# A two-layer hybrid backbone block: the order of instructions taken from another simulation in the framework

## The chip, the cores and the metric

The kernel runs on one core of one Trainium2 chip. The metric is the device time in microseconds (us) of one execution. Three executions of the kernel before gave 1864.18, 1868.44 and 1869.16 us; their median is 1868.44.

## The reference

Two layers run over 512 latent tokens and 256 context tokens of width 1024. In each layer the tokens are normalised and modulated, go through one input projection, and are mixed by four groups of heads side by side; the outputs are concatenated and projected, then a squared-ReLU MLP of width 4096 follows. Layer 2 drops the context after the mixing. Cut to what matters:

```python
for l in range(2):
    mx, mc = modulation(c, ...), modulation(c_ctx, ...)          # 6 rows of 1024 each
    px, pc = norm(x) @ w_in[l], norm(xc) @ w_in[l]               # 1024 -> 3344 columns
    gdn = gated_delta_net(pc, px)       # chunks of 64: a triangular solve, then a chain over chunks, both directions
    sc  = short_conv(px)                # gate * conv3(gate * x)
    hy  = hyena(px)                     # x0 * longconv(x1 * v), filters from a small MLP, by a Fourier transform
    na  = neighbourhood_attention(pc, px)   # softmax over a window and the context
    x = x + mx[2] * norm(concat(gdn, sc, hy, na) @ w_out[l])
    x = x + mx[5] * norm(square(relu(norm(x) @ w1[l])) @ w2[l])
    # layer 1 does the same for the context
```

## The kernel before, in words

Every large product is made of three matmuls on values that are split into a high and a low part (`mm3`, L135 to L140). A weight block of 128x512 comes by DMA into one of three `raw` buffers (`raw`, L116), ScalarE writes its high part `whi` (L126) and VectorE its low part `wlo` (L127), each in a ring of four. `big` (L146) makes one block of 128 output columns of the input projection or of the first MLP product: 12 matmuls of 512 columns on PSUM tile `mx` and 12 of 256 on `mc` for every such weight block in layer 1.

The stages of a layer follow each other in the source, and in the main in the trace:

1. Hyena: `hyena_project`, the filter spectra (`spectrum`, `spectra`; GpSimd makes `ha` at L472 and L473, and the matmuls of L508 and L521 read it), `hyena`.
2. DeltaNet, preparation: `gdn_rates`, `gdn_project` for k and q (each block goes through `dwconv`, L377 to L386, on ScalarE and VectorE), `gdn_normalise`.
3. DeltaNet, solve: `gdn_solve`. `gdn_inverse` (L853) first gathers the diagonal blocks (L866) and transposes them (L870), then runs 30 rounds of a product and an addition on VectorE (L886 and L888), each waiting for the one before it; `gdn_levels` builds the rest of the inverse with small matmuls (L932 to L981). As fill for TensorE, `values()` traces three blocks of the attention's projection (`na_project`, GpSimd splits them at L1137 and L1138) and the projection of v behind `gdn_inverse`.
4. DeltaNet, chain: `gdn_run` steps both directions of `gdn_chain` (L988 to L1088) in turn, six chunks each, across TensorE, ScalarE, VectorE and GpSimd.
5. `gdn_gate` and the rest of `na_project`, then `na_heads` (scores, softmax, values), `gdn_out`, `short_conv`.
6. `mlp`: the output projection, the norm, and the MLP in 11 groups of blocks.

The rows of the modulation are one more stream, spread over all of layer 1: `mod_steps` (L247) loads a 512 KB block of weights (L254) and reduces it on VectorE with up to four multiply-and-accumulate instructions (L258); 80 blocks in all. `step_mods` traces so many of them at chosen places, and in the MLP `mods` (L1403) ties each behind a given VectorE instruction with `issue_after`.

What sets the order: the source traces the instructions with the framework's tile context. When the context closes (L1709, L1710), the framework's scheduler plays the traced program on a simulated machine. Whenever an engine of that machine can take an instruction, it takes, among those whose inputs and buffers are ready by simulated time, the one traced first. The order in which each engine took its instructions becomes the order in the program, and the chip keeps it: an instruction whose inputs are late holds up all behind it on its engine or queue. Where the source says `issue_after`, an instruction stays behind a named one. SyncE's one queue (SP) issues all DMAs in such a fixed order. The framework has two simulated machines: a plain one, used without an argument, and a timeline simulation, which its own text calls the more detailed of the two.

## Time and profile before

| | |
|---|---|
| runs | 1864.18, 1868.44, 1869.16 us, median 1868.44 |
| profiled execution | 1861.5 us; its span 1859.7 us |
| busy | TensorE (PE) 1772.7 us, 95%; its weight loads (PEld) 1436.0; VectorE (DVE) 1267.8; ScalarE (ACT) 774.3; GpSimd (POOL) 263.1 |
| mean granted TensorE clock | 0.986 of full speed |
| DMA | 233.55 MB, 126 GB/s mean |

The span runs from the first to the last instruction; 1.8 us of the execution lie outside it. Matmuls are pipelined, so a busy PE row says that PE had work, not that it ran at its peak. A wait is put down to the engine whose semaphore came last. The granted clock is 1.00 at the upper of TensorE's two levels and 0.5 at the lower, averaged over a stretch.

### The profile page before, as it was taken

The numbers are of one execution on the slowest core, as the hardware profiler recorded it, in microseconds if no ns is written. First come the engines' busy times: TensorE is split into PE (matmuls) and PEld (weight loads), VectorE is DVE, ScalarE is ACT, GpSimd is POOL, SyncE is SP. The second block draws the span as 40 slices with busy tenths as digits, with TensorE's granted clock in tenths as the row PEclk, the third lists the DMA queues.
The fourth block names the chain that finished last, engine by engine and source line by source line (L and its number), as shares of the span: only waits on it lengthen the run. The fifth ranks groups of instructions, "written<-read, shape, count | busy, mean of one in ns | idle before, by whom it ended". The sixth has DMA issues, their size and how long they took to land. (4 is left out here: it accounts for less than half of the span.)

```text
span 1859.7 us, 29504 instructions
## 1 busy us (share of the span) xinstructions
PE 1772.7 (95%) x11170; PEld 1436.0 (77%) x11170; DVE 1267.8 (68%) x2366; ACT 774.3 (42%) x1548; POOL 263.1 (14%) x273
## 2 busy tenths in 40 slices
PE   6899888999999999999999999988899999999998
PEld 2667777788889888888888866777687787777776
DVE  5889898767776777655555586789756765544545
ACT  6333643466565222212222363463347662332323
POOL 0202531600120000000000041162330110000002
PEclk9999999999999999999999999999999999999999
DMA  8452213353565443433444233212235653322322
GB/s 300 150 182 97 91 63 114 118 147 124 182 212 170 146 129 117 123 124 114 130 125 131 83 141 111 69 60 91 73 103 152 210 182 98 106 98 78 115 80 85
DMA packets 105346, 233.55 MB, mean 126 GB/s; under 512 B 13202, under 2 KB 18132, under 8 KB 103925
## 3 DMA queue, kind: packets, MB, share of 16 engines
q1 hardware_dynamic: 105204, 231.68, 38.4%
q8 instruction: 88, 1.44, 0.3%
q14 instruction: 54, 0.43, 0.1%
HBM read 208.42 MB, written 23.21 MB: 125 GB/s over the span
## 5 line engine op out<-in xcount | busy, mean ns | idle before, releaser
L126 ACT CAST whi<-raw 128x512 fp32r<-128x512 f32 x444 | 273.6, 620 | 666.9 <-PE pb L140 269.8
L127 DVE TENSOR_TENSOR wlo<-raw,whi 128x512 fp32r<-128x512 f32 x444 | 317.1, 720 | 216.2 <-ACT whi L126 210.1
L140 PE MATMUL pb<-acth,wlo 128*128 128x512 f32 (+2 forms) x808 | 282.1, 349 | 0.2 <-DVE wlo L127 0.2
L139 PE MATMUL pb<-actl,whi 128*128 128x512 f32 (+2 forms) x808 | 281.8, 349 | 0.0
L138 PE MATMUL pb<-acth,whi 128*128 128x512 f32 (+2 forms) x808 | 280.9, 348 | 0.0
L138 PE MATMUL pb<-whi,hid 128*128 128x512 f32 x628 | 249.7, 398 | 0.8 <-ACT whi L126 0.6
L139 PE MATMUL pb<-wlo,hid 128*128 128x512 f32 x628 | 248.6, 396 | 0.3 <-DVE wlo L127 0.2
L140 PE MATMUL pb<-whi,hid 128*128 128x512 f32 x628 | 248.7, 396 | 0.0
L1498 DVE TENSOR_TENSOR acc<-acc,pb 128x1024 f32<-128x1024 f32 x96 | 117.2, 1221 | 152.6 <-PE pb L140 151.5
L258 DVE SCALAR_TENSOR_TENSOR junk<-adrow,cbc 128x512 bf16<-128x512 f32 x256 | 181.7, 710 | 6.0 <-DMA adrow<-in_adaD_dram 2.9
L139 PE MATMUL mx<-actl,whi 128*128 128x512 f32 x416 | 172.3, 414 | 1.4 <-POOL actl L374 1.2
L140 PE MATMUL mx<-acth,wlo 128*128 128x512 f32 x416 | 171.7, 413 | 0.5 <-DVE wlo L127 0.4
L138 PE MATMUL mx<-acth,whi 128*128 128x512 f32 x416 | 168.8, 406 | 2.1 <-ACT acth L235 1.2
L138 PEld LDWEIGHTS pb<-acth,whi 128*128 128x128 f32 x808 | 152.1, 188 | 20.4
L140 PEld LDWEIGHTS pb<-acth,wlo 128*128 128x128 f32 x808 | 152.0, 188 | 20.1 <-DVE wlo L127 0.4
L139 PEld LDWEIGHTS pb<-actl,whi 128*128 128x128 f32 x808 | 151.8, 188 | 20.1
L374 POOL TENSOR_TENSOR actl<-et,acth 128x256 fp32r<-128x256 f32 (+2 forms) x64 | 56.2, 896 | 732.7 <-DVE et L373 728.5
L138 PEld LDWEIGHTS pb<-whi,hid 128*128 128x128 f32 x628 | 117.8, 188 | 33.0 <-ACT hid L1399 5.4
L140 PEld LDWEIGHTS pb<-whi,hid 128*128 128x128 f32 x628 | 117.8, 188 | 29.5 <-DVE hid L1400 1.8
L139 PEld LDWEIGHTS pb<-wlo,hid 128*128 128x128 f32 x628 | 117.8, 188 | 28.3 <-DVE wlo L127 1.1
L138 PEld LDWEIGHTS mx<-acth,whi 128*128 128x128 f32 x416 | 79.5, 191 | 19.1 <-ACT acth L235 1.6
L139 PEld LDWEIGHTS mx<-actl,whi 128*128 128x128 f32 x416 | 79.7, 192 | 18.3 <-POOL actl L374 1.9
(398 smaller groups left out, 3015.3 us busy)
## 6 DMA issues: line engine op xcount, KB each, us to landing
raw<-in_w_dram SPq DMA_DIRECT2D x276, 256.0 KB, 2.8
adrow<-in_adaD_dram SPq DMA_DIRECT2D x80, 512.0 KB, 3.7
raw<-in_win_dram SPq DMA_DIRECT2D x104, 256.0 KB, 2.6
raw<-in_wout_dram SPq DMA_DIRECT2D x64, 256.0 KB, 3.0
X<-xdr SPq DMA_DIRECT2D x14, 512.0 KB, 4.4
X<-in_xin_dram SPq DMA_DIRECT2D x12, 512.0 KB, 5.1
xdr<-X SPq DMA_DIRECT2D x10, 512.0 KB, 2.8
adp<-in_adaP_dram SPq DMA_DIRECT2D x16, 256.0 KB, 5.5
```

The lines of the kernel that those rows point to most:

```text
L126: self.nc.scalar.copy(hi, raw)
L127: self.nc.vector.tensor_sub(lo, raw, hi.bitcast(F32))
L138: mmul(o, st[0], mv[0], start=first, stop=False)
L139: mmul(o, st[0], mv[1], start=False, stop=False)
L140: mmul(o, st[1], mv[0], start=False, stop=last)
L258: nc.vector.scalar_tensor_tensor(self.junk, raw[:, hs], 1.0, self.cbc[:, cnd, hs], op0=OP.mult, op1=OP.mult, accum_out=self.part[:, l, cnd ...
L374: nc.gpsimd.tensor_sub(lo[:, r], t, hi[:, r].bitcast(F32))
L1498: op = nc.vector.tensor_add(o, o, ps)
```

## The change

The tile context is opened with one more argument. Nothing that is traced changes: not an instruction, a tile, a buffer count, a priority or an `issue_after`. The scheduler plays the same traced program on the framework's timeline simulation in place of its plain one, and the order of every engine and of the DMA queue comes from there.

```diff
-    with tile.TileContext(nc) as tc:
+    with tile.TileContext(nc, schedule_with_timeline_sim=True) as tc:
         Net(tc, aps).run()
```

## Rows read from the trace of the kernel before

**Rows 1.** Busy time of each engine by stage, from the windows: x counts instructions.
```profile
0.00:60.00 60.00, 44.07 (x201) 21.06 (x201) 35.00 (x90) 35.81 (x66) 7.54 (x12) 1.00 0.78 283
60.00:250.00 190.00, 172.85 (x1032) 137.93 (x1031) 169.04 (x324) 82.92 (x182) 56.61 (x38) 0.97 0.33 115
250.00:326.00 76.00, 66.66 (x946) 57.14 (x947) 67.90 (x109) 25.59 (x45) 12.53 (x11) 0.91 0.31 102
326.00:372.00 46.00, 43.67 (x642) 36.68 (x639) 32.83 (x87) 18.67 (x37) 28.79 (x42) 1.00 0.38 115
372.00:558.00 186.00, 183.25 (x1097) 151.69 (x1096) 131.54 (x287) 118.75 (x256) 25.18 (x32) 1.00 0.53 166
558.00:1069.00 511.00, 511.00 (x2555) 429.59 (x2554) 325.99 (x663) 143.84 (x272) 0.00 (x0) 1.00 0.41 126
1069.00:1210.00 141.00, 130.92 (x657) 99.69 (x657) 102.48 (x163) 65.09 (x126) 35.18 (x32) 0.96 0.30 106
1210.00:1340.00 130.00, 113.06 (x1243) 93.55 (x1241) 114.48 (x177) 58.77 (x132) 45.74 (x40) 0.95 0.23 78
1340.00:1534.00 194.00, 188.31 (x1453) 154.74 (x1453) 124.80 (x249) 121.17 (x251) 40.22 (x61) 1.00 0.50 156
1534.00:1813.00 279.00, 278.79 (x1189) 222.27 (x1188) 139.70 (x183) 87.44 (x148) 0.00 (x0) 1.00 0.30 96
1813.00:1860.00 47.00, 40.08 (x175) 31.65 (x174) 24.09 (x40) 16.27 (x36) 11.31 (x8) 0.96 0.24 84
```

**Rows 2.** What PE waited for: us in total, times, longest us.
```profile
PE mc L138 <- DVE cv L385: 10.1, 2, 5.2
PE zp L932 <- DVE diagT L897: 7.9, 2, 4.4
...
PE dps L508 <- POOL ha L472: 5.8, 2, 3.0
...
PE dps L521 <- POOL ha L472: 2.9, 1, 2.9
```

**Rows 3.** VectorE's groups of instructions from 251 to 297 us, layer 1's solve.
```profile
L886 DVE TENSOR_TENSOR prod<-sys 128x60 f32<-128x60 f32 (+14 forms) x30 | 16.6, 553 | 0.7
L888 DVE TENSOR_TENSOR sys<-sys,prod 128x60 f32<-128x60 f32 (+14 forms) x30 | 15.7, 525 | 0.8
L127 DVE TENSOR_TENSOR wlo<-raw,whi 128x512 fp32r<-128x512 f32 x9 | 6.2, 689 | 1.4 <-ACT whi L126 1.3
```

**Rows 4.** VectorE in order of time, where the recurrence begins.
```profile
250.69 0.72 DVE L383 SCALAR_TENSOR_TENSOR cv<-mx,conv,cv 128x511 f32<-128x511 f32 x1
251.32 0.26 DVE L886 TENSOR_TENSOR prod<-sys 128x60 f32<-128x60 f32 x1
251.48 0.75 DVE L385 SCALAR_TENSOR_TENSOR cv<-mx,conv,cv 128x511 f32<-128x511 f32 x1
252.13 0.26 DVE L888 TENSOR_TENSOR sys<-sys,prod 128x60 f32<-128x60 f32 x1
```

**Rows 5.** The modulation's accumulations (L258) around the solve: window, length, VectorE busy.
```profile
250.00:297.00 47.00, 0.00 (x0) 0.92 0.26 89
326.00:372.00 46.00, 13.85 (x32) 1.00 0.38 115
```

**Rows 6.** What the DMA queue (SP) waited for: us in total, times, longest us.
```profile
SPq L118 <- DVE wlo L127: 757.4, 385, 11.7
...
SPq L629 <- DVE ub L628: 47.6, 6, 17.9
SPq L1133 <- ACT na L1131: 45.5, 4, 15.4
```

**Rows 7.** A table load on ScalarE and the instruction behind it, in order of time.
```profile
252.31 1.28 ACT L644 ACT_TABLE_LOAD   x1 [5.90 <-DVE cv L385]
253.60 0.63 ACT L644 ACTIVATE cv<-cv 128x512 f32<-128x512 f32 x1
```

## The prediction

> **What bounds the kernel now.** I read the windows by stage first. PE is busy for 1772.65 of the 1859.7 us, so it idles for 87, and the rows say where: 511.00 busy of 511 in layer 1's MLP and 278.79 of 279 in layer 2's, 790 us in which the order can save nothing; 15.9 idle at the start, where DMA moves 283 GB/s; 17.2 from 60 to 250; 9.3 and 2.3 in layer 1's solve and chain; 2.8 up to the MLP; 10.1, 16.9 and 5.7 in layer 2's three stretches before its MLP; 6.9 at the end [rows 1]. The granted clock is 1.00 but for 0.97 and 0.91 from 60 to 326, 0.96 and 0.95 from 1069 to 1340 and 0.96 at the end: TensorE is at its lower level for part of the stretches in which it also idles [rows 1]. In those stretches VectorE has little room: 169.04 of 190, 67.90 of 76, 114.48 of 130 us busy [rows 1].
>
> Then the list of PE's waits, to see whether the present order makes PE wait for something late while other work stands ready. The longest are few and are true dependences at the borders of stages: 10.1 us in two waits for `dwconv` (VectorE was gathering the inverse's diagonals first), 7.9 for the transposed result of the recurrence, 5.8 and 2.9 for GpSimd's `ha` [rows 2]. That is 26.7 us of the 87, and the trace shows no crowd of short, misplaced waits behind them.
>
> **The change part by part.** Nothing is added or removed; all instructions, DMAs and buffers stay. Only the order can move, and it can move on every engine and on SP's queue. The trace of before can't show the new order, so each place where two streams share an engine gets a bound from both sides and a value.
>
> (a) The recurrence on VectorE. It is what ends last in the solve: 30 products of 16.6 us and 30 additions of 15.7 in layer 1, 32.3 us of work in the 44 us from its first to its last instruction, and in between come other VectorE instructions, of which nine `wlo` of 0.69 are the largest group with 6.2 us [rows 3]. They alternate one by one with the links of the chain, because at each link the other stream was ready when the next link was not [rows 4]. So what the new simulation says about readiness decides how many slip in. From below: all others out, 44 - 32.3 = 11.7 us less per layer, 23 us in both, if PE still has fill. From above: the modulation's accumulations, of which none runs in the solve now and 16 (with their 16 accumulator reads 13.85 us) run right behind it [rows 5], all move in, +13.9 us, in layer 1 alone, and nine more `wlo` in each layer, 2 x 6.2, +26.3 together. I take half of the 16 accumulations, +6.9, and three more `wlo` in layer 2, 3 x 0.69 = +2.1; the choice lies toward the upper end because a lower-placed instruction that is ready is always taken and never held back for a link that will be ready soon. What is behind the recurrence is `diagT`, and PE already waits for it (7.9 us in the two layers [rows 2]): a later recurrence comes out at PE's wait nearly whole.
>
> (b) The border stalls. From below all 26.7 us go [rows 2]; from above they double. I take 0: these waits are for results which the traced priorities put late (the diagonals before `dwconv`), and the priorities don't change.
>
> (c) SP's queue. Loads wait for a free `raw` buffer as a rule (757.4 us in 385 waits), and some stand behind a store whose data is late, 17.9 us at the longest behind `ub`, 15.4 behind `na` [rows 6]. In the present order this costs PE next to nothing in the MLPs, as the four `whi`/`wlo` pairs cover it. Below: 0, there is nothing to win there. Above: if the ring runs dry as in the stretch from 1340 to 1534, where PE idles 5.7 of 194 us [rows 1], 2.9% of 790 us, 23 us. I take 0, the MLP's own row.
>
> (d) Start, chain, attention and end. PE idles 15.9 + 2.3 + 2.8 + 5.7 + 6.9 us there [rows 1]. Some 10 us of the start are loads that no order hides; I let these stand at 0, between -10 and +10, for either order fills the chain from the same projections.
>
> (e) Loads of activation tables. Each costs ScalarE 1.28 us, and the next ACTIVATE starts 1.29 us after the load did [rows 7]. An order that lets a Silu or a square root in among the exponentials pays twice for each visit. There are six such visits to the attention stage (four Silu of the gates, two square roots in `gdn_out`), 12 loads, 15.4 us of ScalarE, in stretches where it is busy for 118.75 of 186 and 121.17 of 194 us [rows 1]: cover for all of it. I take 0, -2 to +5. The Trainium skill ("ScalarE: Activation LUTs", section "What ACT_TABLE_LOAD costs") puts a switch at 1283 ns plus a drain of about 1380, 2.66 us together; by that the 12 would be an estimated 32 us. This trace agrees with the first figure and shows no drain between the load and the next instruction.
>
> The sum: 1861.5 + 6.9 + 2.1 = 1870.5 for an execution like the profiled one, which was 6.9 us below the median of the three runs; carried to the median, **1877 us**, 0.5% slower.
>
> **The rivals.** A change within 0.3%, 5.6 us, is about what can't be told from none.
>
> *Faster.* The new simulation's times fit the chip better, so that the fill arrives where PE now waits. For it: the waits of 5 us each for `dwconv` are the same at the same place in both layers [rows 2], a sign of a systematic error rather than of chance, and TensorE's clock falls in the same stretches. Against it: PE has only 87 us of idle time, of which the start, the end and the MLPs hold 23, and VectorE is busy for 88 to 89% where the rest is [rows 1]. If the two waits for `dwconv` and half of the other border waits go (10.1 + 8.3), it is 1868.4 - 18 = 1850.
>
> *No difference that counts.* The order differs only where it is free to differ, or not at all where the long chains and PSUM buffers tie it; then the argument does not do what it says. For it: 790 us are PE-bound, and the traced priorities stay. Against it: the alternation in the recurrence depends on ready times of tenths of a us [rows 4]. 1868 us.
>
> *Much slower.* The fill is put ahead of the chain of the solve in both layers: the one mechanism is a VectorE or PE queue which holds ready low-priority instructions when a link of the chain becomes ready. For it: the links already wait for one 0.7 us instruction each [rows 4]; against it: one is the rule in the trace and most of the 60 links wait for none. Each of the 60 links behind one `wlo` would be 60 x 0.69 = 41 us a layer less the 11.7 that are there now; with half of the links so, in both layers, 2 x (20.7 - 11.7) = 18, with PE's fill used up early, so that the chain of 46 us behind it (43.67 busy, part of it fill [rows 1]) runs uncovered at +10 a layer: 38 in all, 1907 us. It decides from the point at which more than a third of the links wait.
>
> **How the numbers follow.** Forecast, slower by 0.3 to 1.5%: 0.35, its own range 1874 to 1896. Faster: 0.31. No difference: 0.24. Much slower: 0.10. So faster 0.31, within 0.3% 0.24, slower 0.45. The range: 1868.4 - 23 = 1845 is the sum with the whole lower bound of (a) and nothing else, and a fifth of the faster case I put below 1843; from above, the upper bounds of (a) and (b) together give 1868.4 + 26.3 + 26.7 = 1921, past the much slower case's 1907. So 1843 to 1921.
>
> **What would show it.** Right: the same instruction counts; the time from the first L886 to the last L888 grows in layer 1, with rows of L258 inside it, and the wait of `zp` for `diagT` with it; both MLPs still without idle time on PE. Wrong: the two waits of PE for `dwconv` gone and the granted clock near 1.00 from 250 to 326 (faster); idle time on PE inside an MLP, with waits for `whi` or `wlo` in front (c was mis-sized); more table loads and PE waiting for ScalarE in the attention (e). If the order differs in the solve and the span doesn't, the recurrence is not what ends last there.

## The result, and the profile after

The changed kernel takes 1939.05 us (median of four, 1936.85 to 1940.65) where the kernel before takes 1866.31 (median of four, 1863.47 to 1869.16): 1.0389 times as long, 95% interval 1.0366 to 1.0412. The profiled execution has 1940.1 us and a span of 1938.2, 78.5 more than before.

The instructions are the same but for seven more loads of activation tables. So the span is PE's busy time and its idle time, and both grew: busy from 1772.7 to 1787.0 us (+14.3), idle from 87.1 to 151.2 (+64.1). The stages show where. First the kernel before, in four stretches of each layer: up to the first product of the recurrence; the recurrence; the levels and the chain; the attention. The columns are those of [rows 1]. The three dots stand for what lies between the two layers' stretches.

```profile
0.00:251.30 251.30, 216.93 (x1231) 158.99 (x1231) 205.34 (x415) 118.72 (x248) 65.39 (x50) 0.98 0.44 155
251.30:295.10 43.80, 40.39 (x221) 35.32 (x221) 40.32 (x78) 14.24 (x26) 5.65 (x4) 0.92 0.26 90
295.10:366.40 71.30, 64.33 (x1281) 53.46 (x1283) 53.95 (x104) 26.17 (x51) 32.44 (x45) 0.95 0.32 106
366.40:453.20 86.80, 86.20 (x659) 70.72 (x653) 59.34 (x155) 61.66 (x143) 6.18 (x11) 1.00 0.52 142
...
1094.60:1261.70 167.10, 152.82 (x840) 118.83 (x838) 122.61 (x188) 79.51 (x172) 58.52 (x48) 0.96 0.25 86
1261.70:1308.10 46.40, 40.36 (x200) 33.98 (x200) 43.28 (x81) 15.11 (x27) 7.45 (x6) 0.93 0.31 101
1308.10:1371.60 63.50, 58.61 (x1185) 47.75 (x1187) 40.57 (x73) 25.52 (x50) 24.03 (x41) 0.97 0.17 58
1371.60:1429.80 58.20, 56.73 (x444) 44.95 (x438) 40.66 (x90) 41.09 (x92) 6.71 (x11) 1.00 0.57 161
```

The same eight stretches of the kernel after:

```profile
0.00:282.80 282.80, 256.67 (x1443) 195.66 (x1444) 217.22 (x431) 133.50 (x275) 60.13 (x49) 0.99 0.43 147
282.80:327.90 45.10, 35.63 (x192) 30.19 (x192) 41.69 (x76) 8.43 (x16) 9.21 (x7) 0.92 0.33 112
327.90:418.50 90.60, 76.65 (x1371) 64.92 (x1370) 63.24 (x129) 29.98 (x55) 32.22 (x43) 1.00 0.27 84
418.50:497.00 78.50, 55.98 (x411) 40.70 (x408) 52.82 (x153) 52.45 (x126) 5.40 (x11) 0.78 0.57 146
...
1131.90:1347.50 215.60, 207.58 (x1129) 167.57 (x1130) 143.40 (x218) 104.31 (x215) 69.64 (x59) 0.96 0.28 96
1347.50:1388.50 41.00, 25.22 (x108) 19.72 (x106) 39.48 (x79) 7.21 (x12) 2.39 (x2) 0.85 0.26 84
1388.50:1452.00 63.50, 46.52 (x1124) 40.72 (x1126) 37.47 (x67) 22.52 (x43) 23.50 (x41) 0.80 0.05 16
1452.00:1505.50 53.50, 39.68 (x345) 32.66 (x342) 31.90 (x76) 36.27 (x83) 5.33 (x11) 0.81 0.52 142
```

Length less PE's busy time is the idle time. Up to the recurrence it fell, from 34.4 to 26.1 us in layer 1 and from 14.3 to 8.0 in layer 2. In the three serial stretches behind it, it rose from 3.4 + 7.0 + 0.6 = 11.0 to 9.5 + 14.0 + 22.5 = 46.0 in layer 1, and from 6.0 + 4.9 + 1.5 = 12.4 to 15.8 + 17.0 + 13.8 = 46.6 in layer 2. These 69 us are more than the whole growth of 64. The recurrence begins 31.5 us later in layer 1, although PE idles less before it: PE did something else first. What, shows in the instructions of one tile, `mx`, which all projection blocks use. Before, the same stretches (PE, PEld, VectorE and ScalarE, then clock and DMA):

```profile
0.00:251.30 251.30, 94.83 (x349) 62.88 (x349) 15.51 (x21) 9.40 (x14) 0.98 0.44 155
251.30:295.10 43.80, 25.87 (x101) 18.88 (x101) 2.36 (x4) 2.47 (x4) 0.92 0.26 90
295.10:366.40 71.30, 15.45 (x42) 7.90 (x42) 0.00 (x0) 1.17 (x2) 0.95 0.32 106
366.40:453.20 86.80, 36.61 (x121) 20.91 (x121) 16.14 (x27) 17.74 (x50) 1.00 0.52 142
...
1094.60:1261.70 167.10, 90.03 (x340) 62.48 (x338) 14.82 (x20) 9.34 (x14) 0.96 0.25 86
1261.70:1308.10 46.40, 31.12 (x128) 23.56 (x128) 2.98 (x4) 3.03 (x5) 0.93 0.31 101
1308.10:1371.60 63.50, 18.48 (x51) 9.29 (x51) 0.00 (x0) 1.17 (x2) 0.97 0.17 58
1371.60:1429.80 58.20, 26.75 (x97) 17.29 (x97) 13.47 (x20) 12.63 (x33) 1.00 0.57 161
```

After:

```profile
0.00:282.80 282.80, 119.77 (x453) 83.25 (x454) 17.73 (x24) 11.80 (x18) 0.99 0.43 147
282.80:327.90 45.10, 25.09 (x96) 18.56 (x96) 0.69 (x1) 1.76 (x3) 0.92 0.33 112
327.90:418.50 90.60, 19.97 (x77) 13.49 (x75) 1.35 (x2) 0.59 (x1) 1.00 0.27 84
418.50:497.00 78.50, 0.00 (x0) 0.00 (x0) 14.95 (x25) 17.10 (x48) 0.78 0.57 146
...
1131.90:1347.50 215.60, 135.81 (x517) 97.25 (x518) 17.55 (x24) 13.46 (x21) 0.96 0.28 96
1347.50:1388.50 41.00, 25.22 (x108) 19.72 (x106) 2.04 (x3) 0.58 (x1) 0.85 0.26 84
1388.50:1452.00 63.50, 0.00 (x0) 0.00 (x0) 0.00 (x0) 0.00 (x0) 0.80 0.05 16
1452.00:1505.50 53.50, 0.00 (x0) 0.00 (x0) 11.52 (x17) 12.41 (x32) 0.81 0.52 142
```

104 more `mx` matmuls stand ahead of layer 1's recurrence (453 against 349) and 177 more ahead of layer 2's (517 against 340). By the attention, where 121 and 97 stood, none is left; in layer 2 none is left from the levels on. (The counts of VectorE and ScalarE there belong to a tile of the softmax with the same name.) No matmul is added, and the fill is used up before the stages in which it stood.

What PE waited for, over the whole span (us in total, times, longest), and the two MLPs from the windows:

```profile
PE zp L932 <- DVE diagT L897: 21.0, 2, 18.0
PE sc L1199 <- ACT P L1213: 13.1, 8, 4.4
PE mx L140 <- DVE wlo L127: 12.7, 4, 8.5
PE sc L1199 <- DMA nak<-nak: 10.2, 5, 3.2
```

```profile
581.00:1099.00 518.00, 516.58 (x2613) 437.43 (x2613) 333.03 (x681) 150.76 (x287) 11.40 (x16) 1.00 0.41 130
1570.00:1890.00 320.00, 317.69 (x1458) 259.06 (x1458) 165.58 (x233) 114.47 (x201) 7.71 (x8) 1.00 0.33 106
```

Against [rows 2], the two waits of `mc` for `dwconv` (10.1 us) and those for `ha` of L472 (8.7) are gone from the list. In their place stand the recurrence with nothing beside it (18.0 us at once, layer 2), the softmax and the loads of `nak`. The MLPs stay bound by PE.

The recurrence, the rows that answer to [rows 3], layer 1 and 282 to 328 us:

```profile
L888 DVE TENSOR_TENSOR sys<-sys,prod 128x60 f32<-128x60 f32 (+14 forms) x30 | 17.2, 572 | 0.9
L886 DVE TENSOR_TENSOR prod<-sys 128x60 f32<-128x60 f32 (+14 forms) x30 | 16.7, 556 | 0.7
L127 DVE TENSOR_TENSOR wlo<-raw,whi 128x512 fp32r<-128x512 f32 x10 | 7.5, 748 | 1.6 <-ACT whi L126 1.6
```

Its work is nearly as before (33.9 us against 32.3), and so is its company on VectorE: ten `wlo` instead of nine, and no accumulation of the modulation.

PE's busy time, the other 14.3 us, grew while the clock fell. The mean granted clock fell from 0.986 to 0.966; with levels of 1 and 0.5 that is 2 x 0.014 x 1859.7 = 52 us at the lower level before and 2 x 0.034 x 1938.2 = 132 after. Laid over the clock's records, PE is busy in 40 of the 52 and in 76 of the 132. The same 72 matmuls of the attention's scores, before and then after (by form, last column idle time and releasers):

```profile
L1199 PE MATMUL sc<-nak,naq 128*128 128x256 f32 x72 | 20.2, 302 | 0.0
```

```profile
L1199 PE MATMUL sc<-nak,naq 128*128 128x256 f32 x72 | 28.6, 406 | 24.1 <-ACT P L1213 13.1 <-DMA nak<-nak 10.2 <-issue 0.5
```

302 ns became 406, in a stretch whose clock is 0.78 in layer 1 and 0.81 in layer 2, where it was 1.00. That is 8.4 us. The Trainium skill ("TensorE: Matmul & The Clock Gate", section "HAM oscillation — how this bites in real kernels") puts the cost of throttled time at half of it; by that 80 us more would be an estimated 40. This trace shows 14.3: PE had something to run in only 36 of the 80 us.

### The profile page after: what moved, and what is told of

Same layout as the page of the kernel before. It is cut to its first block, busy times and chain, and to the rows that moved or that the text cites. A ratio compares the mean times of both kernels' runs of the same rounds, so it can differ in the third digit from the quotient of the medians.

```text
span 1938.2 us, 29529 instructions
## 1 busy us (share of the span) xinstructions
PE 1787.0 (92%) x11170; PEld 1459.7 (75%) x11170; DVE 1275.9 (66%) x2366; ACT 780.7 (40%) x1555; POOL 258.8 (13%) x273
## 4 chain that ended last, share of the span: by engine, by line
PE 66%; DVE 13%; DMA 7%; ACT 5%; issue 5%; POOL 1%; SPq 1%; DVEq 0%; ACTq 0%; POOLq 0%
PE pb L139 15%; PE pb L140 15%; PE pb L138 15%; PE mx L138 3%; PE mx L140 3%; PE mx L139 3%; DVE wlo L127 2%; DMA adrow<-in_adaD_dram 2%; DVE junk L258 1%; DMA raw<-in_wout_dram 1%; DMA raw<-in_w_dram 1%; DVE prod L886 1%; ACT whi L126 1%; DVE sys L888 1%; PE mc L139 1%
## 5 line engine op out<-in xcount | busy, mean ns | idle before, releaser
L127 DVE TENSOR_TENSOR wlo<-raw,whi 128x512 fp32r<-128x512 f32 x444 | 322.1, 731 | 241.8 <-ACT whi L126 237.2
L138 PE MATMUL pb<-whi,hid 128*128 128x512 f32 x628 | 248.6, 396 | 1.2 <-ACT hid L1399 1.2
L140 PE MATMUL pb<-whi,hid 128*128 128x512 f32 x628 | 241.8, 395 | 0.0
L258 DVE SCALAR_TENSOR_TENSOR junk<-adrow,cbc 128x512 bf16<-128x512 f32 x256 | 181.3, 708 | 20.9 <-DMA adrow<-in_adaD_dram 17.9
L140 PEld LDWEIGHTS mx<-acth,wlo 128*128 128x128 f32 x416 | 80.1, 192 | 31.9 <-DVE wlo L127 15.0
```

The costliest lines, as they stand in the source:

```text
L127: self.nc.vector.tensor_sub(lo, raw, hi.bitcast(F32))
L138: mmul(o, st[0], mv[0], start=first, stop=False)
L140: mmul(o, st[1], mv[0], start=False, stop=last)
L258: nc.vector.scalar_tensor_tensor(self.junk, raw[:, hs], 1.0, self.cbc[:, cnd, hs], op0=OP.mult, op1=OP.mult, accum_out=self.part[:, l, cnd ...
```

## The experiments

Times are medians; the kernel before, run beside them each time, had 1864.5 to 1867.4 us. All stand on the two kernels of the diff.

**Holding the fill back (e1, e2, e3).** The timeline simulation stays, and `issue_after` on TensorE ties fill behind a named instruction: in e1 all fill behind the last product of `gdn_systems`, in e2 `short_conv` behind the chain, in e3 both. The lines shown are from e3.

```diff
             self.gdn_inverse(UX, p, ip)
-            values()
+            with self.tc.issue_after(self.sys_last):
+                values()
...
-                self.short_conv(l, w_in[20:26], hx, segs, y[2:4])
+                with self.tc.issue_after(self.chain_last):
+                    self.short_conv(l, w_in[20:26], hx, segs, y[2:4])
```

> The kernel after, but every TensorE instruction of the fill (the projection of v, the gates, the attention's projections, short_conv) is queued behind the last product of gdn_systems, so none can be taken before or inside it. Fill theory (the 73 us are fill that is used up before the serial stages and missing beside them): the first L886 comes 30 us (layer 1) and 45 us (layer 2) earlier, recurrence and chain are covered, the attention stays bare as in the kernel after (PE idle there 22.5 and 13.8 us, clock 0.8); 1895 to 1915 us. Queue theory (ScalarE, VectorE and the DMA queue in a worse order, fill or no fill): the waits stay where they are, over 1925 us.

1979.4 us (ratio 1.060, 1.058 to 1.063): a miss, and in the other direction. Layer 1's recurrence did come early (246.9 us), but the fill that was held then went into levels and chain (244 and 240 `mx` matmuls in the two layers), and the attention stayed bare: 2 and 0 there, PE idle for 18.5 and 13.4 us.

> The kernel after, but short_conv's TensorE instructions are queued behind the last instruction of the chain (gdn_run), so they stand beside the attention; all other fill is as in the kernel after. Fill theory: the attention's idle time (22.5 and 13.8 us) goes and its clock returns to 1.00, but recurrence, levels and chain lose the blocks that were there, some 30 us of fill a layer in the solve alone; no gain overall, 1930 to 1980 us. Queue theory: the attention keeps its waits for nak loads and P, and the solve is as in the kernel after; 1930 to 1945 us with the idle time still in the attention.

1957.7 us (1.050, 1.048 to 1.052), as expected: PE idles 7.2 and 3.6 us in the two attentions (22.5 and 13.8 without the hold), and 26.7 and 32.8 us in the two recurrences (9.5 and 15.8). Where the fill stands, PE is covered, and where it was taken away, PE waits:

```profile
PE zp L934 <- DVE diagT L899: 75.4, 4, 40.3
```

That is the wait of L932 for L897; it was 21.0 us in the kernel after.

> Both holds together: no fill before the end of gdn_systems, short_conv behind the chain; all other orders still from the timeline simulation. Fill theory: nearly all of the loss comes back, 1860 to 1885 us, with PE idle under 100 us and a mean clock of at least 0.98. Queue theory: most of the loss stays, over 1910 us.

1944.5 us (1.043, 1.041 to 1.045). Not better than the change itself; the expectation fell. The head of PE's waits in e3 says why:

```profile
PE fTps L763 <- DVE ktok L735: 30.8, 2, 15.7
```

The normalisation before the systems needs fill too: with all of it held, PE stands some 15 us in one piece there, once in each layer.

**Fill first under the plain simulation (e4).** The kernel before; `values()` is only traced ahead of `gdn_systems`, and so has the first claim.

```diff
+            values()
             UQ = self.gdn_systems(kT, qT, nq, p, ip)
             UX, qk = UQ[:, :, 0, :], UQ[:, :, 1, :]
             self.gdn_inverse(UX, p, ip)
-            values()
```

> The kernel before with its plain simulation, but the projection of v and the three attention blocks are traced ahead of gdn_systems, so that five blocks of fill have the first claim before the serial stages. Fill theory: the same loss without the timeline simulation: layer 2's chain and attention have no fill left, layer 1's attention about half; 1890 to 1920 us, with lower clock in layer 2's chain and attention. Queue theory: the plain orders of ScalarE, VectorE and the DMA queue are kept, so the time stays within 1% of before, under 1885 us.

1906.3 us (1.023, 1.020 to 1.027), as expected. `mx` by the two attentions of e4:

```profile
397.30:482.10 84.80, 17.50 (x60) 10.64 (x60) 15.23 (x26) 17.11 (x49) 0.92 0.54 144
...
1422.60:1472.50 49.90, 0.00 (x0) 0.00 (x0) 11.53 (x17) 12.16 (x32) 0.90 0.54 143
```

60 and 0 instead of 121 and 97, a clock of 0.92 and 0.90, and 26.8 us more idle time on PE in levels, chain and attention of both layers. Fill taken early costs up to 41 us without any timeline simulation; 29 table loads instead of 21 are in that figure too.

**Orders pinned engine by engine (e5 to e8).** The program is traced twice. The first trace is scheduled by one simulation; of the second, scheduled by the other, the instructions of chosen engines are chained in the first one's order.

```diff
+    nc, traced = build(FROM)
+    nc, _ = build(not FROM, [order(nc, traced, e) for e in PINNED])
...
+            for a, b in zip(order, order[1:]):
+                tc.add_manual_dep(ins[names[b]], names[a], dep, reason="pinned")
```

> Timeline simulation for all engines and the DMA queue, but TensorE's order is pinned, instruction by instruction, to the one of the kernel before. Fill theory (what costs is where TensorE's fill stands; e3 failed because it left the normalisation without any): 1860 to 1885 us, no stage with over 6 us more idle time than before. Queue theory (the other engines' and the DMA queue's orders cost by themselves): over 1910 us.

1929.2 us (1.034, 1.031 to 1.036): the fill theory as I held it falls. With TensorE's instructions in their order of before, the kernel is still 62 us slower. Its first stretch, up to the first Silu of k, and its attention:

```profile
0.00:172.90 172.90, 134.89 (x636) 88.29 (x636) 133.12 (x300) 64.20 (x122) 24.25 (x22) 0.91 0.53 185
...
398.70:496.50 97.80, 90.49 (x661) 73.28 (x658) 64.79 (x172) 62.39 (x143) 6.13 (x11) 0.97 0.49 132
```

And the first of the two in the kernel before:

```profile
0.00:156.40 156.40, 130.87 (x672) 86.20 (x673) 119.59 (x252) 64.71 (x123) 25.51 (x21) 0.98 0.54 190
```

The attention has its fill and is 11 us longer all the same. The first stretch is 16.5 us longer, and VectorE has 48 instructions more in it. Those of L258 alone (VectorE, then clock and DMA), in e5 and then in the kernel before:

```profile
0.00:172.90 172.90, 39.06 (x96) 0.91 0.53 185
```

```profile
0.00:156.40 156.40, 18.95 (x52) 0.98 0.54 190
```

44 of the 48 are the modulation: 22 accumulations with their reads, 20 us. But this is e5's own order and not that of the kernel after, for the simulation plays the free engines anew beside the pinned one (e5 has 21 table loads, the kernel after 28). The kernel after comes to its first Silu of k at 135.8 us, earlier than the kernel before, with 40 accumulations (each with its read) on VectorE:

```profile
0.00:135.80 135.80, 30.41 (x80) 0.00 (x0) 0.99 0.64 224
```

So e5 shows that TensorE's order alone does not bring the time back. What the other engines' orders cost in the kernel after itself, it does not show.

> The reverse: the plain simulation for everything, but TensorE's order is pinned to the one of the kernel after. Fill theory: the loss is there without the timeline simulation on any other engine, 1920 to 1950 us, PE idle in the attention of both layers as in the kernel after. Queue theory: under 1890 us.

1993.4 us (1.069, 1.066 to 1.072). With TensorE's order of the kernel after, the two attentions stand bare again, PE idle for 19.1 and 13.0 us, though the plain simulation orders all else; but the whole is slower than either forecast.

> Timeline simulation with the orders of ScalarE, VectorE, GpSimd and the DMA queue pinned to the kernel before; TensorE alone is free to follow the new simulation. If TensorE's order alone is what the new simulation spoils: over 1910 us. If it takes fill early only because the weight blocks of the fill are split early on the other engines (the built order shows 96 mx matmuls back in layer 1's attention, 48 in layer 2's): 1860 to 1885 us.

1999.9 us (1.073, 1.067 to 1.078). That is over 1910, but not by the fill's place: 96 and 72 `mx` matmuls are back in the two attentions.

> Timeline simulation with ScalarE's order alone pinned to the kernel before; all else is free. The built order has 96 mx matmuls back in layer 1's attention and 48 in layer 2's (0 in the kernel after, 94 and 66 in the kernel before). Split theory (which weight block ScalarE splits next decides when fill becomes ready): 1862 to 1890 us. If each engine has its own share in the loss: 1900 to 1930 us. If ScalarE is not in it: over 1930 us.

2030.9 us (1.088, 1.085 to 1.092), although the fill is back by the attention (96 and 60 `mx` matmuls). All three mixtures are slower than either whole order, which no theory had said. The same wait of PE in e6, e7 and e8:

```profile
PE mx L138 <- DVE cv L385: 17.7, 2, 13.7
PE mx L138 <- DVE cv L385: 22.4, 8, 11.3
PE mx L138 <- DVE cv L385: 53.2, 11, 10.4
```

Blocks wait for a PSUM tile that `dwconv` reads late; no such wait of `mx` stands in either whole kernel's list. I read it so, and no run tested it: one engine's queue takes the blocks in one sequence and another's in another, and each waits in order.

**Fill and modulation put back by hand (e9, e10, e11).** e9 holds the fill more finely than e3: three attention blocks are free, the rest goes behind the systems, and the last five (layer 1) or four (layer 2) blocks of `short_conv` behind the chain. e10 ties half of the modulation blocks traced in `gdn_project` behind the spectral products of hyena's first segment, the 512 latent tokens; e11 does both. The diff is e10's.

```diff
-            if l == 0 and nm != "v":
+            if l == 0 and nm == "k":
                 self.step_mods(GPM)
+            if l == 0 and nm == "q":
+                with self.tc.issue_after(self.hy_mid):
+                    self.step_mods(GPM)
```

> The kernel after with the fill placed as in the kernel before, by three kinds of hold on TensorE alone: three attention blocks free, the projection of v, gates and the rest behind gdn_systems, short_conv's last five (layer 1) or four (layer 2) blocks behind the chain. The built order has 312, 164, 28 and 120 mx matmuls before the systems, in the solve, in the levels and by the attention in layer 1 (before: 304, 137, 26, 118). If the place of the fill is all: 1865 to 1890 us. If the modulation's accumulations pulled into hyena (48 before its first spectral product, 26 in the kernel before) cost besides: 1895 to 1925 us. If neither counts for much: over 1925 us.

1915.1 us (1.026, 1.022 to 1.030): 24 us back. The attentions have 120 and 96 `mx` matmuls again (121 and 97 before), so the place of the fill by stage is nearly restored, and 50 us of the loss remain. Of e3's two waits for `ktok` 19.2 us are left:

```profile
PE fTps L763 <- DVE ktok L735: 19.2, 2, 10.4
```

> The kernel after, but the second half of the modulation blocks traced in gdn_project (24 accumulations on VectorE) is queued behind hyena's spectral products, as it stands in the kernel before. Modulation theory: these 24 accumulations of 0.7 us and their reads delay hyena on a VectorE that is full there; hyena ends some 15 to 20 us earlier, and 1915 to 1930 us. If the delay of hyena costs nothing because TensorE is filled meanwhile: 1935 to 1945 us.

1945.8 us (1.043, 1.040 to 1.046): no gain. But the hold did not give these accumulations their place of before. L258 from hyena's first spectral product to hyena's end, in the kernel before and in e10:

```profile
137.10:169.90 32.80, 0.00 (x0) 1.00 0.18 61
```

```profile
153.40:212.30 58.90, 18.19 (x48) 1.00 0.40 127
```

Before, none runs there and 22 follow behind hyena. In e10 the held 24, with their reads, run inside hyena, ahead of and among the products of its second segment, and the stretch takes 58.9 us, where the kernel after takes 43.2. So e10, and e11 and e15 with the same hold, do not tell what the place of before would bring.

> Both holds of e9 and e10 on the kernel after. If the two fillers (TensorE's blocks and VectorE's accumulations) in the wrong places are the cause: 1865 to 1895 us. If the orders of the other instructions and queues cost as much: over 1910 us.

1923.2 us (1.031, 1.028 to 1.034): no gain over e9.

**TensorE's order from before, and more with it (e12 to e15).** As e5, with further engines pinned, and in e15 the hold of e10 on top of e5.

> Timeline simulation, with the orders of TensorE and VectorE pinned to the kernel before; ScalarE, GpSimd and the DMA queue follow the new simulation. If TensorE's and VectorE's orders carry the loss: 1862 to 1885 us. If ScalarE's order or the DMA queue's carries part of it: 1895 to 1930 us, as in e5 (1929).

1887.4 us (1.011, 1.008 to 1.014): beside TensorE's order of before, VectorE's is worth 42 us against the one that the simulation gave it in e5. The two orders together bring back 52 of the 73 us. The first stretch takes 162.3 us, with 26 accumulations in it as in the kernel before.

> As e12 (orders of TensorE and VectorE pinned to the kernel before, the rest from the timeline simulation), with ScalarE pinned as well; GpSimd and the DMA queue alone follow the new simulation. If ScalarE's order carries the last 21 us of e12: 1860 to 1872 us. If the DMA queue's order does: 1880 to 1892 us.

1876.7 us (1.007, 1.005 to 1.009): about half of the remaining 21 us; the intervals of e12 and e13 just overlap. A run with every engine pinned, which would show what pinning itself costs, was not made; the 12 us that are left here speak against much.

> As e12, with the DMA queue pinned in place of ScalarE; GpSimd and ScalarE follow the new simulation. If the DMA queue's order carries the last 21 us: 1860 to 1872 us. If ScalarE's order does: 1880 to 1892 us.

1891.1 us (1.014, 1.012 to 1.016): the DMA queue's order brings nothing while ScalarE's is the other one.

> As e5 (TensorE's order from the kernel before, all else from the timeline simulation, 1929 us), with 24 of the modulation's accumulations queued on VectorE behind hyena's spectral products, so 24 instead of 48 stand ahead of them (26 in the kernel before). If their place is the main part of what VectorE's order costs: 1900 to 1915 us, the gain in the stretch before the first Silu of k. If not: 1922 to 1932 us.

1935.1 us (1.037, 1.035 to 1.040): no gain over e5; the first stretch got 4.5 us shorter and the one behind it 8.1 longer.

**The modulation by itself (e16, e17, e18).** e16 is the kernel before with its 12 blocks traced ahead of hyena. e17 and e18 are the two kernels without layer 1's 24 blocks in the mixing, so their output lacks these sums. The diff is theirs.

```diff
-                raw = self.row_block()
-                nc.sync.dma_start(raw, self.a["adaD"][32 + nb if l else nb - 16])
-                for h in range(2):
+                left_out = l == 0 and i < 5
+                if not left_out:
+                    raw = self.row_block()
+                    nc.sync.dma_start(raw, self.a["adaD"][32 + nb if l else nb - 16])
+                for h in range(0 if left_out else 2):
```

> The kernel before with its plain simulation, but its 12 modulation blocks are traced ahead of hyena instead of inside gdn_project: 38 accumulations stand before the first spectral product (26 in the kernel before, 48 in the kernel after). If accumulations ahead of hyena cost what they take there (12 of 0.7 us and their reads): 1872 to 1882 us. If TensorE has cover: within 0.3% of before.

1879.8 us (1.008, 1.006 to 1.009), as expected: 15 us for 12 more accumulations ahead of the first spectral product (38 instead of 26) and 10 more inside hyena.

> The kernel before without the 24 modulation blocks of layer 1's mixing (their loads and 96 accumulations on VectorE are left out and their sums set to zero; the 56 blocks of the MLP stay). TensorE's order hardly changes. It takes VectorE's second stream out of the mixing: 1845 to 1865 us.

1865.8 us (1.001, 0.9995 to 1.002): the kernel before hides these 96 accumulations, their reads and 24 loads without remainder.

> The kernel after with the same 24 blocks left out. If the place of the accumulations is a main part of the loss, the distance to e17 shrinks from 73 us to 35 to 50. If the distance stays at 62 to 80 us, the modulation is not in the loss, and the place of the fill and the order of the stages' own steps carry it.

1925.6 us (1.032, 1.029 to 1.035). The distance to e17 is 60 us, 13 less than with them (some 7 either way, worked out from the three intervals), and so between the two forecasts: the modulation's place is in the loss, with a sixth or so. All other orders were played anew without it, too.

## Why the prediction was wrong

The sign was right; the size (1877, range 1843 to 1921) was not, and the reason given for it wasn't either.

- **The step that failed is (d)**, "I let these stand at 0, between -10 and +10, for either order fills the chain from the same projections." The rows above show levels, chain and attention of both layers going from 14.0 to 67.3 us of idle time (7.0 + 0.6 + 4.9 + 1.5 before, 14.0 + 22.5 + 17.0 + 13.8 after), +53 where I allowed 10. (9 of the 53 lie in the levels, which (d) does not name.) The projections are the same; that they would still be there by then was assumed. An attention without fill stands bare (e1 and e6: PE idle for 13.0 to 19.1 us), and one with fill hardly does (e2 and e3: 3.3 to 7.2); e4 shows that using it early costs time, up to 41 us. How much of the 73 us hangs on it is not settled: putting the fill back by stage returns 24 (e9), TensorE's whole order 10 (e5).
- **(a) was wrong in kind.** No L258 entered the recurrence (all 48 ran ahead of it in both traces), two more `wlo` did in layer 2 (13 against 11), and from first product to last addition the recurrence took 45.1 us in layer 1 and 41.0 in layer 2, against 43.8 and 46.4. The alternation that (a) read from [rows 4] holds for the beginning only: 18 of VectorE's 78 instructions there are no links. PE's wait for `diagT` grew from 7.9 to 21.0 [rows 2] because PE ran out of work beside it (in e2, with less fill there, it is 75.4), not because the recurrence was late in its own time.
- **(b)**, that the border stalls stay, did not hold for one of them: of the 26.7 us named, 18.8 left the list, and the rest, the wait for `diagT`, grew by 13.1.
- **(c) was right**: 1.4 and 2.3 us of idle time in 518 and 320 us of MLP.
- **(e)**: 28 table loads against 21, each 1.283 us, 9.0 us more on ScalarE; the sum had 0 and a bound of 5. The Trainium skill's 1283 ns for a load ("ScalarE: Activation LUTs", section "What ACT_TABLE_LOAD costs") agrees with every one of them. None of the seven more stands in the attention, where (e) looked for them (three are at L644, two at L836, two at L1103), so PE's 13.1 us of waits for the softmax's `P` are not theirs, and e1, e3 and e9 with 21 loads are 2.6 to 6.0% slower than the kernel before all the same.
- **Absent from the sum**: PE's longer busy time at the lower clock, 14.3 us in all. And the much slower case adds up to 1906, not 1907.
- Of the rivals, "much slower" named the right consequence ("with PE's fill used up early", the chain behind it "runs uncovered at +10 a layer") and hung it on the links of the recurrence. The recurrence did not cause it, and the size was too small by the attention, which I had counted as safe because PE idled 0.6 us there. That it idled so little came with 121 matmuls of fill.

What is settled and what isn't: with TensorE's order from before, the time falls from 1939 to 1929; with VectorE's as well to 1887; with ScalarE's to 1877; what is left, 12 us, lies with GpSimd's and the DMA queue's, or with the pinning. These steps can't be read as each engine's own share: pins on other sets of engines made it worse (e7, e8), and each pin changes the orders of the free engines too. So this much is shown: stages without fill stand idle, and giving it back is worth 24 us. The larger part of the 73 us hangs on orders of several engines that no run took apart. Which VectorE instructions are behind the 42 us is open: the accumulations differ visibly in place, leaving them out is worth 13 us, and the holds of e10 and e15 put them into hyena and not behind it. Why the new simulation takes the fill so early was not tested, nor whether its times are nearer to the chip's.

## What to carry to other kernels

A stage in which TensorE hardly idles may be covered by work that could as well run earlier; before a change of order is priced, count that work by stage (the matmuls of the projections' tile by window), and ask what the stage costs bare. An order is best tried as a whole: three kernels with some engines pinned to one order and the rest played by the other simulation (e6 to e8) were slower here than the worse of the two. Judge another scheduler by stage: less idle time early on (8 and 6 us here) is no gain when it is bought with fill. And look up in the trace where a held instruction went before its run is read as a test: the holds of e10 and e15 moved the accumulations to a third place and not to that of before.

## What was not expected of the hardware

The lower clock level costs far less than its time where TensorE has little to run: 80 us more at 0.5 came with 14.3 us more of busy time, for PE ran in only 36 of them. And 96 accumulations on VectorE (0.7 us each, with their reads and 24 loads of 512 KB) cost nothing measurable in one order (1.001, 0.9995 to 1.002) and 13 us in the other.
